# The sample group's bias: three one-hot tables and their products, or shifted loads from a small table in DRAM

## The chip, the cores and the metric

The kernel runs on one core of a Trainium2 chip. The metric is the device time of one execution in microseconds (us); lower is better. A profile records one execution with every instruction of the engines: TensorE (PE for its products, PEld for its weight loads), VectorE (DVE), ScalarE (ACT), GpSimd (POOL) and SyncE (SP), which in this kernel only issues DMAs. DMAs are issued from the queues of SP, ACT and POOL ("SPq", "ACTq", "POOLq" in the rows) and run on the core's 16 DMA engines.

## The reference

One decoder layer is evaluated for two groups of tokens that share all weights: a prompt of 2048 tokens, and a sample group of 8 batches with 4 new tokens each, which attend to a cache of 1024 past positions. Cut to what matters here:

```python
h = RMSNorm(x) @ w_in            # blocks: qa, ka, va, za | ub, zb | qc, zc | gt (three merge gates)
# branch A: 12 heads x 64, three patterns (window, dilation) = (128, 1), (512, 4), (2048, 16);
#   keys at distances 0, d, 2d .. <= window; T5 bias of 32 buckets from one table rel_bias (32, 12)
s = q . k + rel_bias[bucket(distance), head];  s = -1e30 where the key isn't in the pattern
#   the three patterns' outputs are combined by their softmax denominators
# branch B: GLU -> causal depthwise convolution (31 taps) -> LayerNorm -> swish
# branch C: cross-attention (4 heads x 128) into 256 memory tokens
mix = sum over branches of sigmoid(gate) * ((branch * silu(z)) @ w_proj)
y = x + RMSNorm(mix @ w_out)
```

Outputs are y for both groups and the new rows of the caches. For the sample group the bias of a pattern depends on the head, the token t = 0..3 and the key: distance = 1024 + t − position for the cache, t − t' among the four new tokens.

## The kernel before, in words

All large products are done in fp32 precision from two rounded parts: an operand is split into a high and a low part of type fp32r, and `gemm` (L156 to L163) adds the three products high·high, high·low and low·high. `load_w` loads a block of 128 weight columns (512 KB) and splits it, mostly on POOL (`split_pool`, L54 and L55).

The order of work in `build`:

- `phase_a1`. `stage_x` loads the tokens (pool `xst`), normalizes and transposes them (L127) and keeps them as three thirds in SBUF; thirds 1 and 2 also go to DRAM (`d_x`). Then come the blocks q, k, v, u and qc of w_in (tile `g`), with the convolution of branch B on VectorE (pool `cnv`, tiles `G`, `GS`, `acc`, `st_in`).
- `sweep` (the filler): the other 40 blocks za, zb, zc and gt of w_in (tile `gg`), a third of the tokens at a time, weights loaded from ACT's queue. It is traced after everything else of its stage, and so has the lowest priority: it fills gaps.
- `bias_rows`: makes the negated relative-position bias for the prompt as one row per pattern and head, as a product of `rb` (33 x 12; row 32 is 1e30, the mask) and a one-hot table `c_onehot` (33 x 3 x 384), and stores it in DRAM (`d_ext`).
- `sample_bias`: makes the sample group's tables `sb0`, `sb1`, `sb2`, each [112, 672]. Rows 0 to 47 and 64 to 111 are (head, token) for the first and the second batch of a pair. The 672 columns are 512 keys of the cache (positions 512 to 1023), 128 keys in four groups of 32 (positions 16 m + c), and 32 columns for the new tokens of 8 batches. A table is a product of `rbx` (97 rows: high parts in rows 0 to 32, low parts in rows 64 to 96) and a one-hot table `c_onehot_s[:, p]` of shape 97 x 4 x 672, which is loaded (L684, tile `ohf`), rounded on ScalarE (L686, tile `ohs`), multiplied (L690, tile `S`, 8 products) and copied (L692).
- `memory`: keys and values of the 256 memory tokens (`mt`, `w_mem_kv`), LayerNorm of branch B (`conv_norm`, tile `c`), cross-attention of both groups.
- `sample_attention` uses the tables (L795, L796); `attention` is branch A over the prompt, head by head; `fill(1000)` traces the filler.
- `phase_c`: projections (tile `pg`), merge, output projection (tile `y`), norm and residual.

Nothing orders the engines by hand. A scheduler takes the instructions by priority, which is the order in which they are traced (`later` lowers it), and plans each engine's queue with a model of their durations. On the chip each queue then runs strictly in that order: an instruction that waits holds what is behind it on its engine or its DMA queue. SBUF pools on the right side are laid over the pools that were closed before them; with `reuse_waits="tile"` a tile waits only for the old tiles that it overlaps, without it the pool waits for the whole of what it overlaps.

Of the kernel before, what the change touches and what calls it, by code (L numbers as in the profile page):

```python
# [7 lines left out]
F32 = mybir.dt.float32  # L8
R32 = mybir.dt.float32r
AF = mybir.ActivationFunctionType  # L10
# [6 lines left out]
S = 2048  # L17
# [5 lines left out]
NM = 256  # L23
EPS = 1e-6
# [12 lines left out]
class K:  # L37
# [5 lines left out]
    @contextmanager  # L43
    def later(self, lag):
        """what is traced inside yields to what follows within lag instructions"""
        p = self.tc.cur_priority
        self.tc.cur_priority = p + lag
        yield
        self.tc.cur_priority = p

# [6 lines left out]
    def rsqrt(self, pool, v, shape, tag, n=None, m=128):  # L57
        """v (SBUF) -> v ** -0.5 with one Newton step."""
# [81 lines left out]
    def load_w(self, pool, src, kb, tag="w", q=None, bufs=None, act=False, rp=None):  # L140
        """src: [kb*128, n] in DRAM"""
# [13 lines left out]
    def gemm(self, ps, w, xs):  # L155
        """ps = sum_k w[k].T @ x[k]; w, x pairs of fp32r parts; xs list of (h, l)"""  # L156
# [11 lines left out]
    def phase_a1(self, wp, blocks=None):  # L168
        tc, nc, I, O = self.tc, self.nc, self.I, self.O
        with tc.tile_pool(name="x12", side="right", bufs=1) as xpool, \  # L170
# [15 lines left out]
            # thirds 1, 2 go to DRAM for the second sweep  # L186
# [33 lines left out]
    def chunk(self, kind, j, s, n, w, stg, psg, tag, pst=None, q=None):  # L220
        """128 columns of x @ w_in for n tokens"""
# [37 lines left out]
    def blk_u(self, j, wp, stg, cnv, psg, pst):  # L259
# [6 lines left out]
        # states of the sample group, doubled  # L266
# [31 lines left out]
    def conv(self, j, cnv, pst, G, GS):  # L298
# [21 lines left out]
        # rows of the convolution's state  # L320
# [18 lines left out]
    def bias_rows(self, cpool, pool, psum):  # L339
# [13 lines left out]
        nc.sync.dma_start(self.d_ext, ext)  # L353
        pf = pool.tile([128, 3, 128], F32, name="permf")
# [5 lines left out]
    def bias_tiles(self, hp, pool, psum):  # L360
        """negated bias + mask of two heads, [128 queries, 2, 256 keys] in each pattern's order"""
        nc = self.nc
        out = {}
        for p in range(3):
# [4 lines left out]
            # rows are loaded with the queries reversed: a permutation puts them in the pattern's order  # L369
# [22 lines left out]
    def att_pair(self, hp):  # L392
# [5 lines left out]
        # weights of the three patterns: exp(m_g - M) / sum(exp(m_g' - M) l_g')  # L398
# [31 lines left out]
    def att_head(self, hp, a, Oraw, bias):  # L430
# [23 lines left out]
        for p in (2, 1, 0):  # L454
# [11 lines left out]
            # values: [keys, block, hi | lo] (lo | hi for the second head)  # L466
# [18 lines left out]
        # statistics -> rows in token order  # L485
# [19 lines left out]
    def load_v(self, rv, vrow, p, h):  # L505
# [4 lines left out]
        elif p == 1:  # L510
            # block (s, b): partition (c, i) <- row 16 (32 b + i) + s + 4 c
# [9 lines left out]
    def att_chain(self, p, blks, Q, KH, KL, V, bias, Oraw, a, single=False):  # L521
# [18 lines left out]
        def flush(n):  # L540
# [10 lines left out]
            # products: [(key block, first column in t, first query block, count)]  # L551
# [25 lines left out]
        j = 0  # L577
# [85 lines left out]
    def sample_bias(self, keep, pool, psum):  # L663
        """negated bias + mask of the sample group, rows (batch of two, head, token)"""
        nc, I = self.nc, self.I
        NK, R = 672, 112
        rf = pool.tile([33, HA], F32, name="rf")
        rh = pool.tile([33, HA], R32, name="rh")
        nc.vector.tensor_copy(rh, self.rb)
        nc.vector.tensor_sub(rf, self.rb, rh.bitcast(F32))  # L670
        # rows 0..32 the high parts, rows 64..96 the low parts
        zero = pool.tile([97, R], F32, name="zero")
        nc.vector.memset(zero, 0.0)
        rbx = pool.tile([97, 4, R], R32, name="rbx")
        for t in range(4):
            nc.vector.tensor_copy(rbx[:, t], zero)
            for r in (0, 64):
                for p0, src in ((0, rh.bitcast(F32)), (64, rf)):
                    nc.scalar.activation(rbx[p0:p0 + 33, t, r:r + 48].rearrange("p (h t) -> p h t", t=4)[:, :, t],
                                         src, AF.Copy)  # L680
        self.sbias = []
        for p in range(3):
            of = pool.tile([97, 4, NK], F32, name="ohf", bufs=2)
            nc.sync.dma_start(of, I["c_onehot_s"][:, p])  # L684
            oh = pool.tile([97, 4, NK], R32, name="ohs", bufs=2)
            nc.scalar.activation(oh, of, AF.Copy)  # L686
            tf = psum.tile([128, 2, 512], F32, name="S").rearrange("p a b -> p (a b)")
            for x in range(4):
                for c0, c1 in ((0, 512), (512, NK)):
                    nc.tensor.matmul(tf[:R, c0:c1], rbx[:, x], oh[:, x, c0:c1], start=x == 0, stop=x == 3)  # L690
            bt = keep.tile([R, NK], F32, name=f"sb{p}")
            nc.vector.tensor_copy(bt, tf[:R, :NK])  # L692
            self.sbias.append(bt)

# [1 line left out]
    def sample_attention(self):  # L696
        """Two batches at a time, the first in rows 0..47 and the second in rows 64..111 (head, token). A product
        has the high parts of its left operand in one of these ranges and the low parts in the other; the
        two are added as they leave PSUM."""
# [3 lines left out]
        with tc.tile_pool(name="smp", side="right", bufs=1, reuse_waits="tile") as sp, \  # L703
# [44 lines left out]
            def scores(g):  # L748
                qf = qz.rearrange("p j b r -> p (j b r)")
                for bb in range(2):  # L750
                    b = 2 * g + bb
                    for u in range(2):
                        for c in range(2):
                            # element (j, t) at j * 2 R + bb * R + 64 * (bb ^ c) + 8 j + 4 u + t
# [224 lines left out]
    def soft(self, pool, t, m):  # L979
        """softmax over the free axis of a PSUM tile"""  # L980
# [10 lines left out]
    def sample_cross(self, mp, ps):  # L991
# [4 lines left out]
        # queries of (b, h) in columns 4 (4 b + h) .. of an otherwise empty 128-column block  # L996
# [289 lines left out]
```

## Time and profile before

| | |
|---|---|
| median of 3 runs | 3295.53 us (3293.34 to 3299.57) |
| the profiled execution, from first to last instruction | 3298.7 us |
| TensorE: products / weight loads | 3018.8 us (92%) / 2864.5 us (87%) |
| VectorE, ScalarE, GpSimd | 2027.2 us (61%), 1137.6 us (34%), 1350.5 us (41%) |
| mean granted TensorE clock | 0.958 |
| DMA | 456.75 MB, mean 138 GB/s |
| phase_a1's last product (tile g) | 888 us |
| first use of the sample tables (L795) | 1460 us |
| the filler's products (tile gg) | 888 to 2698 us |
| phase_c's products | from 2700 us |

The profiled execution's own device time isn't listed apart from its span; the span lies 3.2 us above the median of the three runs. In the rows "DVE 5.93 (x14)" is busy time and number of instructions. A row of the timeline has the start, the duration, the engine, the line, the operation, the output and the inputs, and in brackets how long the engine had been idle before and what released it. A wait is shown as "engine, tile, line, <- what released it: total us, times, longest us". Products overlap in TensorE's pipeline: a row's duration is longer than the step from one product to the next.

### The profile page before, as it was taken

To read this page: it belongs to the slowest core of one execution; us is meant where nothing else is said; L and a number is where in the kernel's file an instruction comes from. 1 tells how busy PE (TensorE), PEld (TensorE's weight loads), DVE (VectorE), ACT (ScalarE), POOL (GpSimd) and SP (SyncE) were. 2 spreads that over 40 slices of the span, in tenths; PEclk is the share of its full clock that TensorE was granted. 3 is DMA by queue.
4 is the path that set the end of the run, shared out by engine and by line. 5 is a ranking of instruction groups with operands and counts; after the bars stand their busy time and mean duration, and the time that the engine had idled before them with its cause. 6 is when DMAs were issued, how large, how long until landed. Compare 5 with 4: busy or idle time off the path is not lost. (4 is left out here: it accounts for less than half of the span.)

```text
span 3298.7 us, 55514 instructions
## 1 busy us (share of the span) xinstructions
PE 3018.8 (92%) x20717; PEld 2864.5 (87%) x20717; DVE 2027.2 (61%) x3849; ACT 1137.6 (34%) x2856; POOL 1350.5 (41%) x1048
## 2 busy tenths in 40 slices
PE   6999999999814889999999999999999989999999
PEld 6999999999804889999899999999899977787897
DVE  5396696697504793456554666766676547665563
ACT  5100000010102243324444656656575623222221
POOL 0122221222103654644337565557777544142240
PEclk9999999999957899999999999999999999999999
DMA  6222221121113544446746464556757478656561
GB/s 229 99 88 83 72 60 52 49 73 60 68 45 110 178 144 136 152 142 213 241 132 155 126 148 122 148 140 168 175 129 173 105 225 266 215 174 225 158 200 58
DMA packets 531101, 456.75 MB, mean 138 GB/s; under 512 B 117211, under 2 KB 457505, under 8 KB 529773
## 3 DMA queue, kind: packets, MB, share of 16 engines
q1 hardware_dynamic: 356384, 337.44, 34.9%
q10 hardware_dynamic: 169840, 105.02, 11.2%
q0 software_dynamic: 4608, 10.75, 1.0%
q8 instruction: 164, 2.69, 0.4%
q14 instruction: 105, 0.86, 0.1%
HBM read 335.15 MB, written 117.93 MB: 137 GB/s over the span
## 5 line engine op out<-in xcount | busy, mean ns | idle before, releaser
L161 PE MATMUL gg<-x0h,whi 128*128 128x256 f32 (+1 forms) x2560 | 752.1, 294 | 30.3 <-DVE st L237 18.5
L163 PE MATMUL gg<-x0h,wlo 128*128 128x256 f32 (+1 forms) x2560 | 746.1, 292 | 5.6 <-POOL wlo L55 5.6
L162 PE MATMUL gg<-x0l,whi 128*128 128x256 f32 (+1 forms) x2560 | 745.3, 291 | 0.0
L54 POOL TENSOR_SCALAR whi<-wraw 128x1024 fp32r<-128x1024 f32 x162 | 197.2, 1218 | 1022.1 <-PE g L162 478.4
L161 PEld LDWEIGHTS gg<-x0h,whi 128*128 128x128 f32 x2560 | 498.3, 195 | 38.2 <-DVE st L237 15.3
L163 PEld LDWEIGHTS gg<-x0h,wlo 128*128 128x128 f32 x2560 | 497.6, 194 | 8.4 <-POOL wlo L55 6.5
L162 PEld LDWEIGHTS gg<-x0l,whi 128*128 128x128 f32 x2560 | 498.4, 195 | 2.1 <-issue 0.3
L55 POOL TENSOR_TENSOR wlo<-wraw,whi 128x1024 fp32r<-128x1024 f32 x162 | 457.1, 2823 | 10.5 <-PE gg L163 0.9
L311 DVE SCALAR_TENSOR_TENSOR acc<-G,cw,acc 128x1536 f32<-128x1536 f32 (+15 forms) x354 | 460.1, 1332 | 0.0
L150 POOL TENSOR_TENSOR clo<-craw,chi 128x768 fp32r<-128x768 f32 (+1 forms) x96 | 174.9, 1823 | 355.2 <-ACT chi L149 344.8
L601 ACT ACTIVATE P<-T,stm 128x128 f32<-128x128 f32 (+1 forms) x576 | 260.6, 454 | 137.4 <-DVE stm L599 83.3
L161 PE MATMUL pg<-ac,chi 128*128 128x512 f32 (+1 forms) x640 | 229.1, 360 | 14.3 <-ACT ac L1179 6.4
L599 DVE CUSTOM_DVE_ANT_0 T<-s,bias 128x128 f32<-128x128 f32 (+1 forms) x576 | 191.3, 357 | 82.9 <-PE s L591 48.2
L163 PE MATMUL pg<-ac,clo 128*128 128x512 f32 (+1 forms) x640 | 228.2, 358 | 6.6 <-POOL clo L150 6.6
L162 PE MATMUL pg<-ac,chi 128*128 128x512 f32 (+1 forms) x640 | 228.6, 357 | 1.9 <-DVE ac L1180 1.9
L230 ACT ACTIVATE st<-g 128x384 f32<-128x384 f32 (+1 forms) x132 | 60.2, 460 | 447.3 <-PE g L163 447.3
L163 PE MATMUL g<-x0h,wlo 128*128 128x384 f32 x544 | 186.2, 345 | 23.2 <-POOL wlo L55 23.2
L162 PE MATMUL g<-x0l,whi 128*128 128x384 f32 x544 | 187.7, 345 | 0.0
L161 PE MATMUL g<-x0h,whi 128*128 128x384 f32 x544 | 186.0, 343 | 1.0 <-ACT st L230 0.6
L163 PE MATMUL g<-x1h,wlo 128*128 128x384 f32 x544 | 186.3, 342 | 0.0
L162 PE MATMUL g<-x1l,whi 128*128 128x384 f32 x544 | 185.5, 341 | 0.0
L161 PE MATMUL g<-x1h,whi 128*128 128x384 f32 x544 | 183.1, 340 | 2.4 <-ACT x1h L130 2.4
(332 smaller groups left out, 7482.1 us busy)
## 6 DMA issues: line engine op xcount, KB each, us to landing
wraw<-in_w_in ACTq DMA_DIRECT2D x119, 512.0 KB
d_g<-st ACTq DMA_DIRECT2D x168, 128.0 KB
cb<-d_cf SPq DMA_DIRECT2D x72, 256.0 KB
g<-d_g SPq DMA_DIRECT2D x72, 256.0 KB
wraw<-in_w_in SPq DMA_DIRECT2D x35, 512.0 KB
kvc<-in_cache_k_win SPq DMA_DIRECT2D x8, 1536.0 KB
kvc<-in_cache_v_win SPq DMA_DIRECT2D x8, 1536.0 KB
raw<-d_q SPq DMA_DIRECT2D x48, 256.0 KB
```

Source lines behind the costliest of these rows:

```text
L54: nc.gpsimd.tensor_scalar(hi, raw, 1.0, 1.0, op0=ALU.mult, op1=ALU.mult)
L55: nc.gpsimd.tensor_sub(lo, raw, hi.bitcast(F32))
L150: nc.gpsimd.tensor_sub(lo, raw, hi.bitcast(F32))
L161: nc.tensor.matmul(ps, hi[:, k, :], h, start=k == 0, stop=False)
L162: nc.tensor.matmul(ps, hi[:, k, :], l, start=False, stop=False)
L163: nc.tensor.matmul(ps, lo[:, k, :], h, start=False, stop=k == kb - 1)
L230: nc.scalar.activation(st[:, :n], p[:, :n], AF.Copy, scale=sc)
L311: nc.vector.scalar_tensor_tensor(a3[:, lo:hi], G[:, src:src + hi - lo, 2 - m:130 - m], w, a3[:, lo:hi], op0=ALU.mult, op1=ALU.add)
L599: nc.vector.tensor_tensor_reduce(sc[:, :w], t[:, o:o + w], bias[:, 256 - w:256], 1.0, 3.0e38, ALU.add, ALU.min, m)
L601: nc.scalar.activation(P[:, o:o + w], sc[:, :w], AF.Exp, bias=m, scale=-1.0, accum_out=self.stl[:, col:col + 1])
```

## The change

- `bias_rows` moves from the stage after `phase_a1` to the front of `phase_a1`, right behind `stage_x`, in a pool `brw` that lies where `xst` lay (no tile-wise reuse), with PSUM from `phase_a1`'s transposes (`pst`, tile `tr`). The tables `d_x` go out after it in traced order.
- In it, a second one-hot table `c_onehot_s`, now 33 x 3 x 752 (about 290 KB), is loaded once and multiplied by `rb` in six fp32 products of 376 columns; the result `exs` (12 heads x 3 x 752) goes to DRAM as `d_exs`. Its row p holds the bias at falling distances: 515 columns for the cache, 7 for the new tokens, and 230 more of which 32 are filled, for the third pattern, and only there.
- `sample_bias` loses the 97-row tables, their rounding, the 24 products, `rbx` and its 16 small ScalarE instructions, and the pools `brw` and `psb` at that place. It now fills each table with the mask (or zero, for the third pattern) and reads 12 rows (heads) at a time from `d_exs`, shifted by the token: per pattern, half and token one load of 512 columns and one of 4, in the third pattern also one of 128: 56 loads on SP's queue. The four columns of the new tokens are copied to the 8 batches.
- It is now traced after `memory()`, not before it.

```diff
             for _ in st:
                 pass
-            # thirds 1, 2 go to DRAM for the second sweep
+            with tc.tile_pool(name="brw", side="right", bufs=1) as bp:
+                self.bias_rows(self.cpool, bp, pst)
...
         nc.sync.dma_start(self.d_ext, ext)
+        ohs = pool.tile([33, 3, NT_S], F32, name="ohs")
+        nc.sync.dma_start(ohs, I["c_onehot_s"])
+        exs = pool.tile([HA, 3, NT_S], F32, name="exs")
+        for p in range(3):
+            for c in range(0, NT_S, NT_S // 2):
+                cs = slice(c, c + NT_S // 2)
+                t = psum.tile([128, 512], F32, name="tr")
+                nc.tensor.matmul(t[:HA, :NT_S // 2], rb, ohs[:, p, cs], start=True, stop=True)
+                nc.vector.tensor_copy(exs[:, p, cs], t[:HA, :NT_S // 2])
+        nc.sync.dma_start(self.d_exs, exs)
...
-    def sample_bias(self, keep, pool, psum):
+    def sample_bias(self, keep):
...
-            for r in (0, 64):
-                for p0, src in ((0, rh.bitcast(F32)), (64, rf)):
-                    nc.scalar.activation(rbx[p0:p0 + 33, t, r:r + 48].rearrange("p (h t) -> p h t", t=4)[:, :, t],
-                                         src, AF.Copy)
         self.sbias = []
         for p in range(3):
-            of = pool.tile([97, 4, NK], F32, name="ohf", bufs=2)
-            nc.sync.dma_start(of, I["c_onehot_s"][:, p])
-            oh = pool.tile([97, 4, NK], R32, name="ohs", bufs=2)
-            nc.scalar.activation(oh, of, AF.Copy)
-            tf = psum.tile([128, 2, 512], F32, name="S").rearrange("p a b -> p (a b)")
-            for x in range(4):
-                for c0, c1 in ((0, 512), (512, NK)):
-                    nc.tensor.matmul(tf[:R, c0:c1], rbx[:, x], oh[:, x, c0:c1], start=x == 0, stop=x == 3)
             bt = keep.tile([R, NK], F32, name=f"sb{p}")
-            nc.vector.tensor_copy(bt, tf[:R, :NK])
+            nc.vector.memset(bt, 1.0e30 if p < 2 else 0.0)
+            nw = keep.tile([R, 4], F32, name=f"sn{p}")
+            nc.vector.memset(nw, 0.0)
+            base = self.d_exs[:, p, :]
+            for r in (0, 64):
+                for t in range(4):
+                    rows = slice(r + t, r + 48, 4)
+
+                    def src(o, n):
+                        return bass.AP(tensor=base.tensor, offset=base.offset + o, ap=[[base.ap[0][0], HA], [1, n]])
+                    nc.sync.dma_start(bt[rows, 0:512], src(3 - t, 512))
+                    nc.sync.dma_start(nw[rows, :], src(515 + 3 - t, 4))
+                    if p == 2:
+                        nc.sync.dma_start(bt[rows, 512:640], src(522 + 32 * (3 - t), 128))
+            nc.vector.tensor_copy(bt[:, 640:NK].rearrange("p (b t) -> p b t", t=4), nw[:, None, :].to_broadcast([R, 8, 4]))
             self.sbias.append(bt)
...
                     with tc.tile_pool(name="sbk", side="right", bufs=1, reuse_waits="tile") as sk:
-                        with tc.tile_pool(name="psb", side="right", bufs=1, space=PSUM, reuse_waits="tile") as psb, \
-                                tc.tile_pool(name="brw", side="right", bufs=1, reuse_waits="tile") as bp:
-                            self.bias_rows(cp, bp, psb)
-                            self.sample_bias(sk, bp, psb)
                         self.memory()
+                        self.sample_bias(sk)
                         self.sample_attention()
...
+        self.d_exs = t("d_exs", [HA, 3, NT_S])
```

On the host the table of constants is made to match (33 x 3 x 752 in place of 97 x 3 x 4 x 672).

More of the change, by code (lines that the diff above doesn't have):

```diff
@@ L23 @@
 NM = 256
+NT_S = 752
 EPS = 1e-6
@@ L661, in conv_norm @@
             yield
-    def sample_bias(self, keep, pool, psum):
-        nc, I = self.nc, self.I
+    def sample_bias(self, keep):
+        nc = self.nc
         NK, R = 672, 112
[L667 to L676, printed above, removed]
-            for r in (0, 64):
-                for p0, src in ((0, rh.bitcast(F32)), (64, rf)):
-                    nc.scalar.activation(rbx[p0:p0 + 33, t, r:r + 48].rearrange("p (h t) -> p h t", t=4)[:, :, t],
-                                         src, AF.Copy)
@@ L1247, in host_consts, with put @@
             perm[127 - q, p, (q % nr) * (128 // nr) + q // nr] = 1.0
-    pos = np.concatenate([np.arange(512, 1024), (np.arange(4)[:, None] + 16 * np.arange(32)[None]).reshape(-1)])
-    ohs = np.zeros((97, 3, 4, 672), np.float32)
-    for p, (w, d) in enumerate(((128, 1), (512, 4), (2048, 16))):
-        for t in range(4):
-            for x in range(672):
-                dist = 1024 + t - pos[x] if x < 640 else t - (x - 640) % 4
-                ok = 0 <= dist <= w and dist % d == 0
-                k = int(buckets(np.array([dist]))[0]) if ok else 32
-                ohs[k, p, t, x] = ohs[64 + k, p, t, x] = 1.0
+    ohs = np.zeros((33, 3, NT_S), np.float32)
+    ohs[32] = 1.0
+    def put(p, x, dist):
+        w, d = ((128, 1), (512, 4), (2048, 16))[p]
+        if 0 <= dist <= w and dist % d == 0:
+            ohs[32, p, x] = 0.0
+            ohs[int(buckets(np.array([dist]))[0]), p, x] = 1.0
+    for p in range(3):
+        for x in range(515):
+            put(p, x, 515 - x)
+        for x in range(7):
+            put(p, 515 + x, 3 - x)
+    for m in range(32):
+        put(2, 522 + 96 + m, 1024 - 16 * m)
     sm = np.zeros((112, 4, 32), np.float32)
```

## The prediction

> **What bounds the kernel now.** I read the page first: the shares of the engines and the forty slices.
>
> ```profile
> span 3298.7 us, 55514 instructions
> PE   6999999999814889999999999999999989999999
> ```
>
> A slice is 82.5 us. TensorE is busy for nine tenths or more almost everywhere, but in the slices that begin at 907 and 990 us it falls to 1 and 4. Everything else in the kernel is a TensorE stream with small gaps, so this hole is the place to look at. Second view: busy time by stage, cut at the edges of the hole (columns: stretch, length, then busy us and number of instructions of PE, PEld, DVE, ACT, POOL; clock, DMA share, GB/s). The fourth and fifth rows count the products of the filler (tile gg) alone.
>
> ```profile
> 888.00:1022.00 134.00, 23.13 (x108) 17.77 (x106) 5.93 (x14) 11.24 (x23) 2.88 (x2) 0.56 0.14 46
> 1022.00:1100.00 78.00, 58.84 (x409) 57.07 (x410) 58.67 (x57) 24.26 (x39) 41.78 (x38) 0.83 0.48 151
> 1100.00:2698.00 1598.00, 1529.18 (x12195) 1491.55 (x12194) 975.33 (x2454) 816.69 (x2286) 934.12 (x836) 0.98 0.57 157
> ...
> 888.00:1022.00 134.00, 11.85 (x72) 11.39 (x72) 0.75 (x2) 1.02 (x3) 0.56 0.14 46
> 2640.00:2698.00 58.00, 52.24 (x400) 50.71 (x399) 0.00 (x0) 6.36 (x16) 1.00 0.77 217
> ```
>
> In 134 us the machine did 72 useful products, and the granted clock fell to 0.56. After 1100 TensorE is 96% busy (1529 of 1598 us) up to where the filler ends, and the last 58 us of that stretch are filler almost alone. So the stretch ends when the total of products is done, and time saved in the hole moves the end forward: nothing behind it waits for a fixed date.
>
> Third view: who waits for whom between 885 and 1030 us (total us, times, longest), and the large loads in the list of DMAs of that window.
>
> ```profile
> ACT ohs L686 <- DMA ohf<-in_c_onehot_s: 118.6, 3, 41.4
> PE S L690 <- ACT ohs L686: 108.8, 3, 37.7
> ohf<-in_c_onehot_s SPq DMA_DIRECT2D x3, 1018.5 KB
> c<-d_c SPq DMA_DIRECT2D x3, 768.0 KB
> wraw<-in_w_mem_kv SPq DMA_DIRECT2D x3, 512.0 KB
> wraw<-in_w_in ACTq DMA_DIRECT2D x3, 512.0 KB
> mt<-in_mem_prompt SPq DMA_DIRECT2D x2, 512.0 KB
> ```
>
> The products of the tables wait 108.8 us for the rounding on ScalarE, and that waits 118.6 us for three loads of 1018.5 KB; the other four kinds of load are what memory() and the filler need at their start. Fourth view: the instructions in order of time on SyncE's queue, ScalarE and TensorE, which show how the loads hold up the rest (start, duration, engine, line; in brackets the idle time before and its releaser).
>
> ```profile
> 891.35 9.74 SPq L684 DMA_DIRECT2D ohf<-in_c_onehot_s  x2
> 901.19 41.38 SPq L334 DMA_DIRECT2D out_conv_p<-sr  x1
> 949.13 39.88 SPq L145 DMA_DIRECT2D wraw<-in_w_mem_kv  x2
> 1022.96 1.35 SPq L895 DMA_DIRECT2D mt<-in_mem_prompt  x2
> ...
> 932.76 2.44 ACT L686 ACTIVATE ohs<-ohf 97x2688 fp32r<-97x2688 f32 x1 [40.52 <-DMA ohf<-in_c_onehot_s]
> 971.87 2.44 ACT L686 ACTIVATE ohs<-ohf 97x2688 fp32r<-97x2688 f32 x1 [36.67 <-DMA ohf<-in_c_onehot_s]
> 971.88 1.07 ACTq L145 DMA_DIRECT2D wraw<-in_w_in  x2
> 1016.27 2.44 ACT L686 ACTIVATE ohs<-ohf 97x2688 fp32r<-97x2688 f32 x1 [41.41 <-DMA ohf<-in_c_onehot_s]
> ...
> 1018.77 2.74 PE L690 MATMUL S<-ohs,rbx 97*112 97x512 f32 x8 [37.68 <-ACT ohs L686]
> ```
>
> The three tables arrive at 932.8, 971.9 and 1016.3 us, 39 and 44 us apart: 1018.5 KB in 39 us is 27 GB/s. A DMA share of 0.06, one sixteenth, is what a single engine gives:
>
> ```profile
> 900.00:940.00 40.00, 4.12 (x10) 2.03 (x10) 1.40 (x2) 2.44 (x1) 0.00 (x0) 0.51 0.06 27
> 1030.00:1040.00 10.00, 9.77 (x65) 9.54 (x65) 8.68 (x12) 4.64 (x8) 2.52 (x2) 0.80 1.12 338
> ```
>
> The table has 97 rows. The same core moves 338 GB/s right after. While the tables pass, SyncE's queue issues almost nothing (41.38 and 39.88 us on single rows), the weights of the filler (ACTq, 971.88) stand behind the second rounding on ScalarE, and TensorE's ordered queue stands at S. Only when the third table has landed are the memory tokens (mt, 1022.96) asked for.
>
> **The change part by part.** The sum goes against the profiled span of 3298.7 us; the median of the runs shown is 3295.53 us, 3.2 us below it, and I carry that difference through.
>
> *Term 1, the tables go.* Three loads, three ACTIVATEs of 2.44 us, 24 products (3 times 2.74 us), three copies of S, 16 small ACTIVATEs for rbx, and psb's three PSUM banks. All lie in the 134 us, on the path. What must still be done of that stretch is the 72 filler products; at full clock one follows another every 0.12 us:
>
> ```profile
> 888.79 0.28 PE L161 MATMUL gg<-x0h,whi 128*128 128x256 f32 x1
> 888.91 0.28 PE L162 MATMUL gg<-x0l,whi 128*128 128x256 f32 x1
> ```
>
> 72 times 0.12 is 8.6 us, so 134 − 8.6 = 125.4 us can go, if memory() starts at 888 as promptly as it did at 1022.
>
> *Term 2, what is late next.* It can't start quite as promptly. In the hole two w_mem_kv loads (949.13) and two w_in loads (971.88) came for nothing. Afterwards these 2 MB are asked for at 888 together with mt and c. At 338 GB/s they cost 6 us. Meanwhile TensorE has the 8.6 us of filler whose weights were loaded early, so the cover is about as long as the wait. Bounds: a gain of 4 us, because the 65 products of 1030 to 1040 took 0.15 us each at a clock of 0.80 where 0.12 would do (2 us), and the ten us before were no better; a loss of 20 us, if the whole burst must land first (three times 768 and six times 512 KB, 5.5 MB, at the 151 GB/s of 1022 to 1100 are 36 us, less 8.6 us of cover and as much again for the products of the next weight). I take 6 us lost, by the rate of the burst's own row.
>
> *Term 3, work that moves to the front.* bias_rows goes from the hole, where it was hidden, to the front of phase_a1, where TensorE is full. It has three fp32 products of a 384-column row, and six of 376 columns are new.
>
> ```profile
> 893.44 0.85 PE L351 MATMUL tr<-oh,rb 33*12 33x384 f32 x2 [1.61 <-DMA oh<-in_c_onehot]
> 898.35 0.81 PE L351 MATMUL tr<-oh,rb 33*12 33x384 f32 x2
> 937.92 1.45 PE L351 MATMUL tr<-oh,rb 33*12 33x384 f32 x2
> 100.00:110.00 10.00, 8.65 (x48) 8.32 (x49) 0.00 (x0) 1.09 (x2) 4.95 (x3) 1.00 0.54 160
> ```
>
> Nine times 0.83 us is 7.5 us (bounds 6, with the 1.35 us of idle time between 100 and 110 filled, and 9 × 1.45 = 13). The nine copies of 12 rows on VectorE are free: it did nothing (0.00) between 100 and 110.
>
> *Term 4, the waits at the front.* Pool brw takes the place of xst, so its loads (rel_bias, two one-hot tables, perm) can go out only after the last transpose of stage_x, and the convolution's pool cnv comes after brw.
>
> ```profile
> L127 PE MATMUL tr<-ident,xt x136: 242/272/476, 15.9 to 94.5; 128*128 128x128 f32 x128, 32*128 32x32 f32 x8
> 94.53 0.37 SPq L268 DMA_DIRECT2D st_in<-in_state_conv  x1
> 94.84 0.18 POOL L265 MEMSET G<- 128x32 f32 x2 [69.54 <-PE tr L127]
> 98.24 2.05 POOL L54 TENSOR_SCALAR whi<-wraw 128x1024 fp32r<-128x1024 f32 x2 [3.21 <-PE g L162]
> 889.21 1.71 SPq L347 DMA_DIRECT2D oh<-in_c_onehot  x1
> ```
>
> st_in and G were waiting for exactly that and will now wait for brw. Chain: 94.5, the loads, nine products (7.5 us), a copy, a store of exs: about 110 us until G is free. Behind G on POOL's queue stand the splits of the first u weights (98.24), behind st_in two transposes. The load of oh, 148.5 KB in 33 rows, took 4.2 us from issue to use; ohs is twice that, some 6 us. TensorE has the u products to do meanwhile, whose buffers reach for two chunks. I take 4 us (bounds 0 and 15, all from 94.8 to 110).
> The Trainium skill, in "DMA: Bandwidth & Descriptors", section "Why a DMA increments its semaphore by 16 and not by 1", says that a DMA uses the largest number of engines up to 16 that divides its outer dimension. By that, 97 rows get one engine (the 27 GB/s agree) and 33 rows eleven, and ohs would land in some 3.4 us, an estimate by the page's 27 GiB/s an engine, and not 6; the sum would then be 2 to 3 us better.
>
> *Term 5, the new sample_bias.* 56 DMAs of 12 rows each (3 patterns, 2 halves, 4 tokens, two loads, and a third in the last pattern), three fills of 112x672, three small ones and three copies. Nearest rows for such small transfers, and the first use of the tables:
>
> ```profile
> L499 SPq DMA_DIRECT2D d_st<-sT x96: 242/300/683, 1830.9 to 2648.2; - x96
> 1897.66 0.31 SPq L401 DMA_DIRECT2D stc<-d_st  x1
> 1900.03 1.33 DVE L403 TENSOR_TENSOR mn<-stc 32x128 f32<-32x128 f32 x1
> L795 POOL TENSOR_SCALAR T<-sb x12: 723/736/1399, 1460.4 to 1618.8; 112x640 f32<-112x640 f32 x12
> ```
>
> 56 issues of 0.30 us are 17 us of SyncE's queue. The tables are first used at 1460, some 440 us after memory() starts, so they can lie in the queue's idle times; the cover is memory() itself. If they were issued ahead of memory's loads they would cost 17 us. VectorE's three copies stand in its ordered queue and wait for the last small load; what is behind them are LayerNorm and the evictions. I take 2 us (bounds 0 and 17; nothing that it does can gain).
>
> *Sum.* −125.4 + 6 + 7.5 + 4 + 2 = −105.9 us: a span of 3192.8 us, 3189.6 us as a median. All bounds at their best give −125.4 − 4 + 6 = −123 (3172), at their worst −60 (3235).
>
> **The rivals.**
> *The small loads in a row (slower).* The four tokens' rows of a table are interleaved with a step of 4. If the order of writes to one tile were kept by ranges of rows, each load would wait on SyncE's queue for the one before. Load to use is 2.4 us (1897.66 to 1900.03): 56 × 2.4 = 133 us. For that to end slower, more than 110 us of it must stand ahead of loads that TensorE waits for: mt, c and w_mem_kv at the start of memory(). Then 3189.6 + 133 − 2 = 3321 us. For it: SyncE held its queue for 40 us at single rows here. Against it: the queue has idle time for 440 us until 1460, and the filler's weights come over ACTq. 4%.
> *No change.* The same mechanism, hidden in part, gives back just the gain. The Trainium skill's "DMA: Bandwidth & Descriptors", "Rules for kernel authors", has a rule against the change: transfers under 64 KB are mostly overhead and should be merged; the new loads have 24 KB and less. The trace prices such a load at 2.4 us, but shows nobody waiting for one after another. 3295 us, 3%.
> *The wait moves to the front.* Term 4 at its upper end and term 3 at 13 us: 3189.6 + 11 + 5.5 = 3206 us. For it: POOL's and TensorE's queues keep their order, and a transfer later than planned stops what is behind it. 17%.
> *The burst at 888 is the next bound.* Term 2 at 20 us, and SyncE's 17 us ahead of it: 3189.6 + 14 + 15 = 3219 us. For it: 1022 to 1100 shows 19 us of idle TensorE with four loads already there. 13%.
> *Better than the sum.* The start of memory() wholly covered and a warm clock: 3172 us. 8%.
>
> **How the numbers follow.** The forecast itself (3178 to 3200 us, terms near the values taken) has 55%, and its time, 3189 us, is the prediction. The range goes from 3165 to 3228 us: it takes in the front and burst cases and most of the better one, and leaves out the two of 7% together and some tails. About 0.2% (6.6 us) is what a measurement of this kernel can tell from none, as the three runs lie 0.19% apart. Faster by more than that: 55 + 17 + 13 + 8 = 93%; within it 2%; slower 5%, the rest of the no-change case being put there.
>
> **What would show it.** Right: no S product from 97 rows, no slice at 1 or 4, TensorE busy over 60% in the first 134 us after phase_a1, mt asked for within 5 us of the last g product, gg ending near 2592 us, and the same length from there to the end (601 us). Term 3 and 4: tr products of L351's kind and the new ones between 95 and 115 us, and phase_a1 ending near 900 us. Term 5: 56 short rows on SyncE's queue in idle time. Wrong: SyncE's queue in long waits at the small loads with TensorE idle, or a new hole after 888 with weights as its releaser, or VectorE waiting long at the copies of nw.

## The result, and the profile after

| | before | after |
|---|---|---|
| median of the runs made together | 3294.44 us (3290.91 to 3299.57, 4 runs) | 3205.44 us (3198.86 to 3206.21, 4 runs) |
| ratio, 95% interval | | 0.9725 (0.9709 to 0.9742) |
| span of the profiled execution | 3298.7 us | 3203.4 us |
| mean granted TensorE clock | 0.958 | 0.974 |

The change saves 89 us in the medians and 95.3 us from profile to profile. The forecast was 105.9 us, a median of 3189.6 us: the direction, the cause and the range held, and the time lies 16 us above the forecast. From profile to profile the miss is smaller, 10.6 us (105.9 − 95.3). The page of the changed kernel has no hole left among its forty slices:

```profile
span 3203.4 us, 55580 instructions
PE   7999999999988899999999999999898989999998
```

The stages of the changed kernel (columns as in the prediction's table: stretch, length, busy us and number of PE, PEld, DVE, ACT, POOL; clock, DMA share, GB/s). The stretches begin at the end of phase_a1; the last one is phase_c:

```profile
898.00:980.00 82.00, 64.52 (x490) 61.90 (x488) 61.05 (x65) 23.83 (x42) 44.67 (x39) 0.91 0.57 171
980.00:1060.00 80.00, 63.87 (x439) 60.72 (x439) 61.90 (x59) 23.43 (x35) 46.22 (x44) 0.85 0.55 170
1060.00:2602.40 1542.40, 1470.64 (x11749) 1432.22 (x11749) 927.21 (x2398) 791.56 (x2254) 889.66 (x793) 0.98 0.56 154
2602.40:3203.40 601.00, 569.57 (x2736) 469.37 (x2736) 348.44 (x503) 160.50 (x248) 170.00 (x94) 0.97 0.59 187
```

For comparison the kernel before, whole and then counted back from phase_c by equal numbers of products:

```profile
888.30:2700.30 1812.00, 1611.58 (x12711) 1566.62 (x12709) 1039.93 (x2524) 853.26 (x2351) 980.60 (x875) 0.94 0.54 148
1098.00:1162.00 64.00, 59.63 (x463) 58.87 (x464) 44.76 (x57) 22.84 (x41) 52.46 (x49) 0.95 0.58 176
1162.00:2700.30 1538.30, 1472.28 (x11749) 1435.18 (x11747) 931.18 (x2400) 795.31 (x2250) 885.48 (x793) 0.98 0.57 156
```

From the end of phase_a1 to phase_c the kernel before took 1812.0 us, the changed one 82.0 + 80.0 + 1542.4 = 1704.4 us: 107.6 us saved. The cut in front lies 9.7 us later (898.0 for 888.3; phase_a1's last products start at 897.7 and 888.3, 9.4 us apart), and phase_c takes 601.0 us for 598.4. 107.6 − 9.7 − 2.6 = 95.3 us. The rows in between tell where something was given back: 439 products took 80.00 us, where the kernel before did 463 in 64.00 us, 60.7 us for 439. By this count that stretch lost 19 us, the long one after it 4 us, and the first gained 131. The first two belong together, though: they are memory()'s start, which is slow in both kernels (in the kernel before it is the stretch from 1022 us in the prediction's second view, 78 us with 58.84 us of products). Together (888.3 to 1162 us before, 898 to 1060 us after) they gained 273.7 − 162.0 = 111.7 us.

### The profile page after: what moved, and what is told of

Same layout as the page of the kernel before. It is cut to its first block, busy times and chain, and to the rows that moved or that the text cites. A ratio compares the mean times of both kernels' runs of the same rounds, so it can differ in the third digit from the quotient of the medians.

```text
span 3203.4 us, 55580 instructions
## 1 busy us (share of the span) xinstructions
PE 3017.2 (94%) x20705; PEld 2856.5 (89%) x20705; DVE 2041.4 (64%) x3854; ACT 1123.3 (35%) x2835; POOL 1349.0 (42%) x1048
## 3 DMA queue, kind: packets, MB, share of 16 engines
q10 hardware_dynamic: 169840, 105.02, 11.5%
```

## The experiments

*Did the hole come from the 97 rows of the tables?* The prediction read from the DMA share of 0.06 that a transfer of 97 rows runs on one engine, and that what stands behind it waits. One kernel takes only the 97 rows away, another adds such transfers to the changed kernel.

**e1_pad**, the kernel before with tables of 112 rows; the same products follow.

```diff
-            of = pool.tile([97, 4, NK], F32, name="ohf", bufs=2)
+            of = pool.tile([112, 4, NK], F32, name="ohf", bufs=2)
...
-            nc.scalar.activation(oh, of, AF.Copy)
+            nc.scalar.activation(oh, of[:97], AF.Copy)
...
-    ohs = np.zeros((97, 3, 4, 672), np.float32)
+    ohs = np.zeros((112, 3, 4, 672), np.float32)
```

> The kernel before, with the three one-hot tables lengthened from 97 to 112 rows (zeros, loaded and not used): the same products, the same rounding, 15% more bytes, only the number of rows of the loads differs. Theory A (a load of 97 rows goes through one DMA engine, and the queues behind it stand): the three tables land within some 15 us of one another in place of 84, the hole of 134 us shrinks to 30 to 45 us, the time is 3190 to 3215 us. Rival B (3 MB of tables, three roundings of 2.4 us and 24 products are what costs, at whatever row count): the hole keeps over 90 us and the time stays at 3260 us or more.

Measured: 3198.26 us (3189.37 to 3204.44), ratio 0.969 (0.9667 to 0.9714). The roundings of the tables in order of time, the loads on SyncE's queue, and the stretch after phase_a1, in this kernel:

```profile
897.91 2.44 ACT L686 ACTIVATE ohs<-ohf 97x2688 fp32r<-97x2688 f32 x1 [6.24 <-DMA ohf<-in_c_onehot_s]
901.86 2.44 ACT L686 ACTIVATE ohs<-ohf 97x2688 fp32r<-97x2688 f32 x1 [1.50 <-DMA ohf<-in_c_onehot_s]
...
890.65 0.89 SPq L684 DMA_DIRECT2D ohf<-in_c_onehot_s  x2
913.85 1.35 SPq L895 DMA_DIRECT2D mt<-in_mem_prompt  x2
...
888.00:928.00 40.00, 31.42 (x185) 26.90 (x184) 9.69 (x26) 16.89 (x32) 13.96 (x9) 0.83 0.93 281
```

The first two tables come 4 us apart, not 39, in a stretch with a DMA share of 0.93, and the memory tokens are asked for at 913.85, not 1022.96. All of the gain is there, with the tables, their roundings and their 24 products in place: 3198 us against 3205 for the change. The Trainium skill, in "DMA: Bandwidth & Descriptors", section "Why a DMA increments its semaphore by 16 and not by 1", has a transfer use the largest number of engines up to 16 that divides its outer dimension; 112 rows get 16 by it and 97 get one, and both runs agree (shares of 0.93 and 0.06). The semaphores in the traces say the same: that of the first 112-row table is counted up sixteen times as it lands (896.79 to 897.89 us), that of the first 97-row table in the kernel before once at its issue and once at its landing (891.80 and 932.74 us).

**e6_dummy**, the changed kernel with three transfers of 97 rows that nobody reads, ahead of memory().

```diff
+                        for p in range(3):
+                            self.nc.sync.dma_start(self.d_dum[p][:, 0:2048], self.d_qc[3][0:97, 0:2048])
                         self.memory()
```

> The changed kernel, with three added transfers of 97 rows of 8 KB (0.79 MB each) from one DRAM tensor to another, which nobody reads, asked for on the queue of SyncE right after the last store of phase_a1. No SBUF, no product, no rounding. Theory A1 (a one-engine transfer holds the queue and that engine for what comes behind it): 29 us each, 88 us for the three; mt and the memory weights land late, a hole of 40 to 90 us comes back, the time is 3245 to 3295 us. Rival (the hole came from the ordered queues of ScalarE and TensorE, which stood at the rounding and the products; transfers of 128 rows pass by beside a one-engine transfer): under 15 us of loss, 3200 to 3220 us.

Measured: 3279.98 us (3274.41 to 3287.97), ratio 0.9946 (0.9925 to 0.9967): four fifths of the gain are gone. SyncE's queue in this kernel, a stretch of the stages, the waits of TensorE and VectorE between 890 and 1010 us, and ScalarE with its queue ("x2" is two issues in one row, which then runs from the start of the first to the end of the second):

```profile
913.80 29.14 SPq L1201 DMA_DIRECT2D d_dum<-d_qc  x1
943.01 30.15 SPq L900 DMA_DIRECT2D mt<-in_mem_prompt  x1
...
920.00:1000.00 80.00, 0.00 (x0) 0.00 (x0) 0.18 (x1) 1.48 (x1) 3.38 (x2) 0.50 0.16 54
...
PE sco L662 <- DVE sm L660: 91.9, 1, 91.9
DVE sm L660 <- ACT sq L658: 92.3, 1, 92.3
...
936.81 61.45 ACTq L146 DMA_DIRECT2D wraw<-in_w_in  x2
998.31 1.48 ACT L658 ACTIVATE sq<-c 128x1536 f32<-128x1536 f32 x1 [95.59 <-DMA d_dum<-d_qc]
```

TensorE does no product for 80 us, though not one instruction of an engine uses these bytes. The third of the added transfers stands on SyncE's queue for 29.14 us and the first load of mt behind it for 30.15 us. TensorE itself waits for ScalarE's square of c (L658), which reads nothing of the added transfers: it stands behind two weight loads of the filler in ScalarE's queue, issued at 936.81 and 997.88 us, and starts right behind the second. The trace's semaphores tell why these loads came so late. The DMAs issued by SyncE and ScalarE share eight completion semaphores, and an issue waits until the transfer that used its semaphore before has landed. The three added transfers land at 936.8, 967.9 and 997.8 us, some 30 us apart (776 KB in 30 us are 26 GB/s), and the two loads wait for the semaphores of the first and the third. So a slow transfer held the others in two ways, on its own queue and by a semaphore that the other queue needed next; no run separates the two.

e1_pad shows the cause: with the number of rows alone changed the hole is gone. e6_dummy shows that three 97-row transfers bring a hole back without any reader; as the same transfers with 112 rows weren't run, the number of rows rests on e1_pad.

*What the 16 us between forecast and result are.* They could be the 56 small loads, ahead of memory's weights on SyncE's queue; or the front, terms 3 and 4; or the order of the queues.

**e2_front**, the kernel before with the new bias_rows at the front of phase_a1, all its nine products and both stores, and the old tables where they were.

```diff
+            with tc.tile_pool(name="brw", side="right", bufs=1) as bp:
+                self.bias_rows(self.cpool, bp, pst)
...
-                            self.bias_rows(cp, bp, psb)
```

> The kernel before, with the whole bias_rows of the changed kernel (the nine products, both stores) at the front of phase_a1, and the old 97-row tables and products in their old place. Theory A (front costs 8 to 9 us on the path, and the hole is the tables' alone): phase_a1's last product near 897 us in place of 888, the hole as long as before or up to 5 us shorter, the time 3297 to 3306 us. Rival (the front cost is hidden, and the loss against the sum lies elsewhere): the end of phase_a1 within 2 us of 888 and 3288 to 3296 us.

Measured: 3306.55 us (3298.9 to 3320.34), ratio 1.0034 (1.0019 to 1.005). The last transposes of phase_a1 here and, for comparison, in the changed kernel (tile trc: number, least, median and longest ns, first and last start):

```profile
L332 PE MATMUL trc<-ident,so x12: 271/272/272, 284.1 to 898.0; 128*120 128x128 f32 x12
```
```profile
L332 PE MATMUL trc<-ident,so x12: 271/272/272, 284.0 to 897.7; 128*120 128x128 f32 x12
```

The front costs 9.7 us of phase_a1 here (898.0 for 888.3), 9.4 in the changed kernel, and shows as 6 to 17 us in the total (0.19% to 0.5%).

**e3_noloads**, the changed kernel without the 56 loads.

> The changed kernel without the 56 small loads: the sample tables keep their fill, so the sample group's bias is left out; bias_rows stays at the front. Theory C (the small loads, 0.70 us each on SyncE's queue and traced behind memory() but issued ahead of its weights, delay mt and the weights and with them the whole memory stage): mt is asked for right behind the last store, the first kv product comes 15 to 25 us earlier than in the changed kernel, the time is 3172 to 3190 us. Rival D (they lie in idle time; the loss against the sum is the front and the plan of the queues): 3196 to 3207 us.

Measured: 3190.17 us (3188.0 to 3195.24), ratio 0.9686 (0.9662 to 0.971), 13 us below the changed kernel run beside it (after_again, below), with intervals that overlap slightly, and between the two theories' numbers. The first product of memory's keys stands at 933.0 us, not 936.0: what the loads delay directly is 3 us, not the 15 to 25 of theory C. As the order of everything else changes with them, the 13 us can't be put down to the loads (see e9 and e10).

**e5_merged**, twelve stores at the front that already hold the shift, and 14 loads of 48 rows in place of 56.

```diff
-        nc.sync.dma_start(self.d_exs, exs)
+        for t in range(4):
+            nc.sync.dma_start(self.d_exs[:, t, :, 0:512], exs[:, :, 3 - t:515 - t])
+            nc.sync.dma_start(self.d_exs[:, t, :, 640:644], exs[:, :, 518 - t:522 - t])
+            nc.sync.dma_start(self.d_exs[:, t, 2, 512:640], exs[:, 2, 522 + 32 * (3 - t):650 + 32 * (3 - t)])
```

> The changed kernel with the 56 loads merged: the rows shifted by the token are stored four times in DRAM at the front of phase_a1 (12 stores there in place of one), and a table is read by 48 rows at a time: 14 loads. Theory C: SyncE's queue gives back some 30 of 39 us in the ramp; 3178 to 3195 us, if the 12 stores at the front cost under 5 us. Rival D: 3198 to 3212 us (the stores at the front make cnv wait longer).

Measured: 3197.77 us (3194.41 to 3203.38), ratio 0.9708 (0.9684 to 0.9733). With after_again at 0.9727 (0.9693 to 0.9762) that isn't told apart from no difference. The 14 loads take 0.39 to 0.42 us of SyncE's queue each in the median, where the 56 take 0.70, and phase_a1's last product starts 2.6 us later than in the changed kernel (900.3 for 897.7) for the twelve stores. So some 30 us of the queue were given back, as theory C had it, and no gain followed that could be told from noise.

**e4_back**, the changed kernel with bias_rows back behind phase_a1, ahead of memory().

```diff
-            with tc.tile_pool(name="brw", side="right", bufs=1) as bp:
-                self.bias_rows(self.cpool, bp, pst)
...
+                        with tc.tile_pool(name="psb", side="right", bufs=1, space=PSUM, reuse_waits="tile") as psb, \
+                                tc.tile_pool(name="brw", side="right", bufs=1, reuse_waits="tile") as bp:
+                            self.bias_rows(cp, bp, psb)
                         self.memory()
```

> The changed kernel, with bias_rows (all of it, the new table too) moved back to the place after phase_a1 and ahead of memory(). Theory A: phase_a1 ends near 888 us again, 9 us earlier; the nine products (some 7 us) lie in the ramp behind it, where TensorE idles 10 to 15 us, and the small loads come later than memory()'s loads; 3190 to 3203 us. Rival (the ramp is as dear as the front: the products stand in TensorE's ordered queue and wait for the table): 3203 to 3215 us.

Measured: 3168.41 us (3165.47 to 3169.29), ratio 0.9604 (0.959 to 0.9619), below what either theory gave it, and the fastest of all the kernels: 37 us better than the change. SyncE's queue, tiles trc and kv, and stages of this kernel:

```profile
890.24 0.89 SPq L898 DMA_DIRECT2D mt<-in_mem_prompt  x2
892.22 6.56 SPq L146 DMA_DIRECT2D wraw<-in_w_mem_kv  x2
...
L330 PE MATMUL trc<-ident,so x12: 271/272/273, 274.5 to 888.2; 128*120 128x128 f32 x12
L162 PE MATMUL kv<-mh,whi x64: 274/283/580, 908.1 to 985.5; 128*128 128x256 f32 x64
...
980.00:1060.00 80.00, 72.95 (x577) 70.84 (x577) 67.27 (x110) 33.15 (x68) 50.61 (x48) 0.98 0.57 176
888.50:2568.40 1679.90, 1599.09 (x12696) 1547.56 (x12694) 1039.24 (x2529) 843.57 (x2332) 968.13 (x874) 0.98 0.57 158
```

phase_a1's last product starts at 888.2 us again, so the front's 9.5 us are back. The stretch to phase_c takes 1679.9 us, 24.5 less than in the changed kernel, and not only at its start: 577 products between 980 and 1060 us, for 439.

*Is that the place of bias_rows, or the order?* Four kernels vary e4_back, one varies the change, and one repeats it. e4_back itself wasn't run again. The kernel before, run beside each group, took 3296.1, 3296.8 and 3297.4 us, so the groups can be compared.

**e8_back_merged**: e4_back and e5_merged together.

> Both edits together: bias_rows back in the gap ahead of memory(), and the 14 merged loads. With the small loads already behind memory()'s own loads, theory C gives little more than bias_rows in the gap alone (3168 us): 3160 to 3172 us. Rival: the 12 stores in the ramp delay what is behind them on SyncE's queue, 3172 to 3185 us.

**e9_back_noloads**: e4_back without the 56 loads.

> bias_rows in the gap, and the 56 small loads left out (the sample tables keep their fill, so the sample group's bias is left out). If front and small loads are two costs that add up (bias_rows moved into the gap was 35 us better than the changed kernel, the loads left out 13 us): 3155 to 3166 us. If the 3168 us of bias_rows in the gap is mostly a lucky order of the queues: 3172 to 3195 us.

**e10_back_smask**: e4_back with one load of 57 KB, the mask of the sample attention, traced in sample_bias and not after it; the work is the same.

```diff
-            smask = sp.tile([R, 4, 32], F32, name="smask")
-            nc.sync.dma_start(smask, I["c_smask"])
+            smask = self.smask
...
         self.sbias = []
+        self.smask = keep.tile([R, 4, 32], F32, name="smask")
+        nc.sync.dma_start(self.smask, self.I["c_smask"])
```

> bias_rows in the gap, and one load of 57 KB (the mask smask) traced in sample_bias and not at the start of sample_attention: the same work, one load earlier, but the planner lays the queues anew (of TensorE's 19400 rows more than half stand elsewhere). If bias_rows in the gap is worth 35 us by its mechanism: 3160 to 3177 us. If the plan decides: somewhere between 3165 and 3200 us, over 10 us from 3168.

**e11_smask**: the changed kernel with the same edit.

> The changed kernel with the same edit, the mask's load traced in sample_bias: the same work. If the plan is worth little: 3197 to 3209 us. If the plan decides over tens of microseconds: over 8 us from 3203 us, either way.

**e12_back_early2**: e4_back with EARLY, the number of the filler's weight blocks that are loaded early, at 2 in place of 1.

> bias_rows in the gap, and two of the filler's weight blocks loaded in phase_a1 in place of one. If the ramp behind phase_a1 still costs TensorE time for want of weights: phase_a1's end unchanged, TensorE busier by 4 to 8 us in the 20 us behind it, 3158 to 3168 us. If the memory stage's chain on VectorE is the bound there: 3165 to 3180 us, and the plan's changes on top.

**after_again**: the changed kernel once more.

> The changed kernel once more, beside the next three on the same chip: 3198 to 3207 us, phase_a1's last product near 897 us, memory()'s first weight product (kv) near 936 us.

| | bias_rows | median us (range) | ratio (95%) |
|---|---|---|---|
| e4_back | behind phase_a1 | 3168.41 (3165.47 to 3169.29) | 0.9604 (0.959 to 0.9619) |
| e10_back_smask | behind | 3188.13 (3182.89 to 3189.99) | 0.9663 (0.9642 to 0.9684) |
| e12_back_early2 | behind | 3191.99 (3190.5 to 3195.3) | 0.9678 (0.9662 to 0.9695) |
| e9_back_noloads | behind | 3202.93 (3196.94 to 3206.74) | 0.9709 (0.9689 to 0.9728) |
| e8_back_merged | behind | 3202.98 (3195.14 to 3212.85) | 0.9733 (0.97 to 0.9765) |
| e11_smask | front | 3196.34 (3184.7 to 3198.33) | 0.9683 (0.966 to 0.9706) |
| after_again | front | 3202.91 (3195.01 to 3217.49) | 0.9727 (0.9693 to 0.9762) |

e10_back_smask does e4_back's work with the same instructions and takes 20 us more; at 15% of the 20705 places in TensorE's queue the traces show a product of another tile (at none between the change and after_again). e9_back_noloads does less than e4_back and takes 35 us more; half of its places differ. e8, e9 and e12 all lie above both of the ranges that were expected for them. So costs that add up don't explain these kernels. The reading left is that a small edit gives the scheduler another order, and that two orders of the same work can lie 20 us apart, as e4_back and e10 do. The other such pair, the change and e11_smask, differs in 48% of the places and by 7 to 9 us, hardly clear of the noise. Two stages, first of e4_back and then of e10_back_smask, show where the 20 us arise:

```profile
1360.00:1560.00 200.00, 193.50 (x1460) 179.98 (x1460) 115.73 (x244) 86.38 (x194) 88.81 (x151) 0.98 0.75 234
1560.00:2560.00 1000.00, 962.00 (x7829) 946.98 (x7828) 629.44 (x1809) 591.83 (x1779) 625.04 (x499) 0.99 0.58 147
```
```profile
1360.00:1560.00 200.00, 185.05 (x1374) 172.96 (x1373) 107.97 (x230) 82.33 (x180) 84.20 (x144) 0.96 0.71 223
1560.00:2560.00 1000.00, 960.71 (x7779) 944.67 (x7778) 626.76 (x1819) 593.58 (x1784) 614.95 (x499) 0.98 0.57 144
```

e4_back is 86 products ahead after the 200 us in which the sample attention begins (its first product stands at 1378.5 us in e4_back, 1387.3 in e10_back_smask), and 50 more by 2560. At 0.12 to 0.13 us each, 136 products are 16 to 18 us; phase_c begins 16.6 us earlier (2568.4 and 2585.0 us). The changed kernel does 1343 products in the same 200 us. Which detail of the order makes e4_back the best is open (which transfer shares a semaphore with which also changes with the order; no run tested that): the five kernels with bias_rows behind phase_a1 lie between 3168 and 3203 us, those with it at the front (the change, e3, e5, e11) between 3190 and 3205 us. For use, e4_back is the version to take; how much of its 37 us is the place of bias_rows is not shown beyond the 9.5 us at phase_a1's end.

## Why the prediction was right, and where its sizes were off

**Term 1, the tables go (125.4 us): right.** The hole is gone, and e1_pad shows the cause: transfers of 97 rows on one engine, with the queues standing behind them. The prediction had read that off a DMA share of 0.06, one sixteenth. (Its row of 39.88 us, read as a single one, holds two issues of 32.30 and 7.40 us.) It didn't draw the consequence: a table of 112 rows would have done.

**Terms 3 and 4, the front (7.5 + 4 = 11.5 us): 9.5 us measured.** The products at the front, with the first work of POOL behind them, in the changed kernel:

```profile
99.33 2.10 PE L354 MATMUL tr<-oh,rb 33*12 33x384 f32 x6
101.90 0.92 PE L364 MATMUL tr<-ohs,rb 33*12 33x376 f32 x2
104.97 3.93 PE L364 MATMUL tr<-ohs,rb 33*12 33x376 f32 x6
113.74 1.43 PE L364 MATMUL tr<-ohs,rb 33*12 33x376 f32 x4
115.23 0.13 POOL L268 MEMSET G<- 128x32 f32 x1 [9.27 <-PE tr L364]
```

Each of the nine products counts as two rows here. They lie between 99 and 116 us, and G was set at 115.2 us, where the prediction had about 110. By its semaphore ohs landed at 100.3 us, 3.8 us after its issue (96.44), nearer the estimate of 3.4 than the 6 taken, and TensorE shows no idle time ahead of the first product from it (101.90).

**Term 2, the burst (6 us lost).** The first 30 us after phase_a1, and two rows that end long waits for transfers, in the changed kernel:

```profile
898.00:928.00 30.00, 18.38 (x113) 16.68 (x112) 20.27 (x23) 8.18 (x14) 13.44 (x8) 0.78 0.74 230
...
909.81 1.06 ACT L902 ACTIVATE msq<-mt 128x1024 f32<-128x1024 f32 x1 [8.55 <-DMA sb<-d_exs]
912.26 1.05 POOL L55 TENSOR_SCALAR whi<-wraw 128x1024 fp32r<-128x1024 f32 x1 [33.93 <-DMA wraw<-in_w_in]
```

TensorE is idle for 11.6 of the 30 us. The tokens mt were used 12 us after phase_a1's end, the filler's next weights after 14. But the sum counted from the start that memory() had at 1022 us in the kernel before, and there TensorE was idle for 7.8 of the first 30 us: the mechanism was there, and in these 30 us it cost some 4 us more than that start. Up to the point from which 11749 products are left before phase_c, the change saved 111.7 us where the sum had 125.4 − 6 − 2 = 117.4, so terms 2 and 5 took 13.7 us together, not 8.

**Term 5, the small loads (2 us, in idle time): the place was wrong, the cost about right.** SyncE's queue in the changed kernel:

```profile
899.71 0.82 SPq L693 DMA_DIRECT2D sb<-d_exs  x1
902.49 0.99 SPq L900 DMA_DIRECT2D mt<-in_mem_prompt  x2
909.75 1.29 SPq L146 DMA_DIRECT2D wraw<-in_w_mem_kv  x2
918.86 0.70 SPq L693 DMA_DIRECT2D sb<-d_exs  x1
957.25 0.70 SPq L696 DMA_DIRECT2D sb<-d_exs  x1
```

An issue takes 0.70 us, not 0.30 (the row of d_st had been taken for it): 39 us of the queue, not 17. They aren't in idle time towards 1460 but the first thing after phase_a1, from 899.7 to 957 us, in between memory's loads. But the loads don't wait for one another, as their issues 0.7 us apart show, which ends the rival of the loads in a row and that of no change. What did wait is ScalarE's queue: by the trace's semaphores (see e6_dummy) its second weight load of the filler waits for a small load that was issued at 903.85 and landed at 909.3 us, and the row of msq, with 8.55 us of idle time before it, stands behind that. In e3_noloads the first of these two weight loads goes out at 900.62 us, in the changed kernel at 907.73. VectorE waited 2.79 us at most at the copies of nw, and memory's first product is only 3 us earlier without the loads.

**Where the sum was short.** Of the 16 us between the medians, 5 are the place of the profiles among the runs: the span before was taken as 3.2 us above the median, and after the change it lies 2.0 us below it. The other 10.6 us are in the profiles: 9.8 between phase_a1's end and phase_c (107.6 us saved, 117.4 in the sum; 5.7 are missing in the first 162 us and 4.1 in the long stretch), 2.6 in phase_c, and the front cost 1.8 less than taken (9.7 for 11.5). So the sentence "time saved in the hole moves the end forward: nothing behind it waits for a fixed date" held but for some 10 us. What it left out is memory() behind the hole, a chain of transposes, norms and evictions with its own pace on VectorE, and the filler waits for its evictions in the same ordered queue. The stage from memory()'s start to some 16 us after its last LayerNorm step and TensorE's waits in it, first in the kernel before, then in the changed one:

```profile
1022.00:1300.00 278.00, 244.59 (x1862) 238.23 (x1863) 203.41 (x265) 104.74 (x191) 158.39 (x143) 0.93 0.50 155
PE gg L161 <- DVE st L237: 16.0, 5, 8.1
PE sco L649 <- DVE sm L647: 3.5, 4, 1.0
...
898.00:1186.00 288.00, 242.11 (x1812) 232.74 (x1811) 212.83 (x274) 100.83 (x188) 151.94 (x141) 0.92 0.50 154
PE gg L162 <- DVE st L240: 20.4, 10, 4.6
PE sco L662 <- DVE sm L660: 12.7, 6, 5.8
```

TensorE is idle for 33.4 of 278 us and for 45.9 of 288 us. The waits for the LayerNorm's sums (sm) grew most, by 9.2 us, those for the filler's evictions (st) by 4.4. An example of the latter, with VectorE and POOL ahead of it, in the changed kernel:

```profile
967.32 12.61 DVE L672 SCALAR_TENSOR_TENSOR c<-sq,c 128x1536 f32<-128x1536 f32 x1 [2.13 <-ACT sq L671]
979.86 0.41 DVE L240 SCALAR_TENSOR_TENSOR st<-st,gg 128x256 f32<-128x256 f32 x1
977.28 1.04 POOL L55 TENSOR_SCALAR whi<-wraw 128x1024 fp32r<-128x1024 f32 x1
980.32 0.58 PE L162 MATMUL gg<-x0h,whi 128*128 128x256 f32 x1 [4.57 <-DVE st L240]
```

One LayerNorm step of 12.61 us holds an eviction of the filler behind it, and TensorE stands for 4.57 us. The kernel before had such a step too, of 11.16 us, and the clock is the same (0.88 in the 162 us, and in the 140 us from 1022 in the kernel before), so neither is what changed. Why the stage waits more in the changed kernel stays open. Its pace isn't fixed: e4_back, in another order, saves 132 us up to phase_c and loses nothing in phase_a1. With 3168 us it reaches the time of the "better than the sum" rival (3172 us), but as another kernel.

The other signs: mt was asked for 4.9 us after phase_a1's last g product had ended (within 5 expected), TensorE was busy for 108.6 of the first 134 us, 81% (over 60% expected), the filler ended at 2600.6 us (2592 expected), and phase_c took 601 us (601 expected). The prediction had no term for the order of the queues, which one pair of runs puts at 20 us. The miss is no larger than that, so that the forecast came this close is in part luck, and the missing 9.8 us behind phase_a1 can be placed but not put down to one cause.

## What to carry to other kernels

When one transfer shows a DMA share of one sixteenth, look at its number of rows first: padding 97 rows to 112 gave what the whole rewrite gave. A slow transfer can cost not only its reader but what is issued behind it, here even on the other queue, so look for long rows on the DMA queues, and for issues that wait for a semaphore of the slow one. And where a scheduler makes the order, estimate how far two orders of the same work lie apart (here up to 20 us of 3200) before a smaller difference is put down to an edit, and before a kernel is kept or dropped for it.

## What the runs showed of the hardware that was not expected

*Three transfers between DRAM tables that nobody reads stopped TensorE.* In e6_dummy two issues stood on SyncE's queue for 29.14 and 30.15 us, about as long as one of these transfers takes (30 us), and TensorE did nothing for 80 us. Part of this is the program's doing: its DMAs share eight semaphores.

*Issues of different forms had different prices.* The loads of 12 rows into every fourth partition take 0.70 us each on SyncE's queue, those of 48 rows into consecutive partitions in e5_merged 0.39 to 0.42 us in the median, the stores of d_st 0.30 us. Number of rows and spacing changed together, so no run tells which of the two counts.

*A short wait of TensorE was paid twice.* Three stretches of 10 us in the changed kernel (columns as above):

```profile
970.00:980.00 10.00, 5.74 (x49) 5.54 (x47) 10.00 (x2) 0.26 (x2) 8.33 (x7) 0.98 0.12 36
980.00:990.00 10.00, 6.47 (x25) 5.71 (x25) 7.31 (x8) 3.90 (x6) 6.75 (x5) 0.50 0.87 261
990.00:1000.00 10.00, 10.00 (x87) 10.00 (x86) 8.20 (x10) 2.23 (x4) 3.31 (x6) 1.00 0.53 150
```

After the 4.57 us of idle time before 980.32 the granted clock is 0.50, and 25 products pass in 10 us where 87 pass in the next ten. The Trainium skill, in "TensorE: Matmul & The Clock Gate", "Part 1: The HAM clock gate", states half rate after an idle window of about 3.4 us; the trace agrees (0.50 after 4.57 us).

*A VectorE instruction with a median of 2.6 us took 12.61 us once, while GpSimd worked.* The group's row (number, least, median and longest ns, first and last start), in the changed kernel:

```profile
L672 DVE SCALAR_TENSOR_TENSOR c<-sq,c x9: 359/2605/12606, 939.1 to 1169.5; 128x1536 f32<-128x1536 f32 x8, 128x192 f32<-128x192 f32 x1
```

The longest ended 1.6 us after GpSimd's row of 977.28 us had ended. The Trainium skill, in "SBUF — State Buffer", section "SBUF: two separate sides", has VectorE instructions with two inputs from SBUF and those of GpSimd that read SBUF lock each other out for whole instructions; the rows fit that, and no run isolates it.
